# Operand addresses, GpSimd's share and the last norm columns of a hybrid decoder layer in float32

## Chip, cores and metric

The kernel runs on one core of a Trainium2 chip. The metric is device time in microseconds, from one execution to the next of the same program; less is better. A profiled execution has its own time, a little above those of the plain runs.

## What is computed

One decoder layer over 256 tokens of width 1,024, all in float32. Five branches read the same input x: block attention (a), a mixture of three dilated windows (b), forgetting attention (c), a gated delta rule (d) and cross-attention into 256 memory tokens (e). Each has six heads of 64 (e has four of 96).

```python
h = x @ w_in + b_in                       # q, k, v, gates z and merge logits of all branches
o = stack([o_a, o_b, o_c, o_d, o_e]) * silu(z)
y = einsum('bsnc,ncd->bsnd', o, w_branch)
y = sum(sigmoid(merge_logits) * y, axis=2) @ w_out
return layer_norm(DEEPNORM_ALPHA * x + y, ln_g, ln_b)
```

In branch b the three windows share one softmax: numerators and denominators of the three groups are added with a common maximum.

## The kernel before

**Split products.** A float32 operand is split into `hi` (rounded, by ScalarE) and `lo` (the rest, by VectorE; `split`, L122), and a product is three matmuls, hi by hi, hi by lo and lo by hi (`mm3`, L126). x is kept split for the whole kernel in `xhi` and `xlo`. Weights are streamed: a `Unit` (L163) loads up to 1,024 columns into a `raw` buffer on SP's queue, splits them into `hi` and `lo`, and its chunks issue the matmuls. A merge cycle has one unit of 24 products with x (256 wide, `mm<-xhi,hi`, `mm<-xhi,lo`, `mm<-xlo,hi`) and one of 9 products with a gated branch, whose operand lies in pool `f3` (`mm<-f,hi`, `mm<-f,lo`); there are five merges of eight cycles. The memory's keys (`mk`) are 72 products of the same width whose operand lies in `big` (`mm<-big,hi`, `mm<-big,lo`).

**Pools.** SBUF is given out in the order in which pools are opened (L79 to L83): `cpool` (constants, `xhi`, `xlo`, small tiles), `wpool` (`raw` x5, `hi` x4, `lo` x4, 4,096 bytes each), `f3` (16 tiles of 3,072 bytes), `big` (2 of 9,216), `sp`.

**Order.** The main loop (L1119) goes through the units. After each chunk `stepper` lets side streams (the attention branches, the delta rule, the memory norm) go on for a few steps. A planner then orders each engine's instructions by its own estimate of times; those passed to `keep` hold their order among themselves.

**The start.** The first four units are the weights of c's values (`wcs`, 402 columns); with each comes a quarter of x (`load_x`, `split_x`, L278 to L289), which takes a `raw` buffer for every two quarters. All loads are on SP's queue.

**Branch b** (`attend`, L724). For each of three head pairs and two heads the exponentials of three score groups are taken on ScalarE with the row sums as accumulators (L768), the three are added up on VectorE (L771), the row sums reduced and inverted (L775, L776), and the result is scaled (L781), transposed on TensorE (L787) and multiplied with v.

**The end.** `load_res` (L1077) loads the residual x and the norm's weights and scales the residual on ScalarE (L1086). The output product of 8 slices (k) is summed in PSUM: token tile 0 in two pieces of 512 columns, tile 1 in 512, 256 and 256 (`PC`, L1021). The pieces of a token tile lie in one two-bank tile (L1036); the last one has its own. `finish` (L1050) issues the last slices piece by piece, adds the residual (L1071), takes statistics (L1072), and `norm` applies the layer norm in two passes of VectorE over each half (L1062, L1063) and stores it.

Of the kernel before, what the change touches and what calls it, by code (L numbers as in the profile page):

```python
# [15 lines left out]
P = 128  # L16
S = 256
# [58 lines left out]
@with_exitstack  # L76
def kernel(ctx: ExitStack, tc: tile.TileContext, T: dict, out: bass.AP):
    nc = tc.nc
    cpool = ctx.enter_context(tc.tile_pool(name="cpool", bufs=1))  # L79
    wpool = ctx.enter_context(tc.tile_pool(name="wpool", bufs=3))  # L80
    f3 = ctx.enter_context(tc.tile_pool(name="f3", bufs=16))
    big = ctx.enter_context(tc.tile_pool(name="big", bufs=2))
    sp = ctx.enter_context(tc.tile_pool(name="sp", bufs=4))  # L83
    ps = ctx.enter_context(tc.tile_pool(name="ps", bufs=2, space=bass.MemoryType.PSUM))
    dr = ctx.enter_context(tc.tile_pool(name="dr", bufs=1, space=bass.MemoryType.DRAM))
# [33 lines left out]
        return pst("av", shape, 1)  # L119


    def split(hi, lo, src):  # L122
        A_.activation(hi, src, AF.Copy)  # L123
        V_.tensor_tensor(lo, src, hi.bitcast(F32), op=ALU.subtract)  # L124

    def mm3(pt, lh, ll, rh, rl, first, last, pin=False):  # L126
# [10 lines left out]
    HR = (slice(0, 64), slice(64, 128))  # L137


    xhi, xlo = ct("xhi", (P, KD, S), F32R), ct("xlo", (P, KD, S), F32R)  # L140
    cst = ct("cst", (P, C_N))
    vb, vcb = ct("vb", (P, 2, BW)), ct("vcb", (P, BW + 18))
    bcol = ct("bcol", (P, T["bcol"].shape[1]))
# [19 lines left out]
    class Unit:  # L163
# [7 lines left out]
        def load(self):  # L171
            self.r = wpool.tile([P, 1024], F32, tag="raw", name=nm("raw"), bufs=NRAW)
            for i, p in enumerate(self.parts):
                if self.before is not None:
                    self.before[0](i, len(self.parts))
                nc.sync.dma_start(self.r[:, p], self.src[:, p])

        def split(self):
            self.h = wpool.tile([P, 1024], F32R, tag="hi", name=nm("hi"), bufs=NHI)
            self.l = wpool.tile([P, 1024], F32R, tag="lo", name=nm("lo"), bufs=NHI)  # L180
            for i, p in enumerate(self.parts):
                if self.before is not None:
                    self.before[1](i, len(self.parts))
                split(self.h[:, p], self.l[:, p], self.r[:, p])

    def need(name):
        while name is not None and name not in done:
# [88 lines left out]
    xraw = {}  # L276

    def load_x(i, j, n):  # L278
        if i % 2 == 0 and j == 0:
            xraw["t"] = wpool.tile([P, 4, S], F32, tag="raw", name=nm("raw"), bufs=NRAW)  # L280
        w = 2 // n
        o = 2 * i + w * j
        xraw[i, j] = xraw["t"][:, o % 4:o % 4 + w]
        nc.sync.dma_start(xraw[i, j], T["xT"][:, o:o + w])

    def split_x(i, j, n):
        w = 2 // n
        o = 2 * i + w * j
        split(xhi[:, o:o + w], xlo[:, o:o + w], xraw[i, j])  # L289

    def evac_c(p, t):
        if t == 0:
# [10 lines left out]
    def consts():  # L303
        for _ in range(CW):
            yield 1
        nc.sync.dma_start(vcb, T["vcb"].to_broadcast([P, BW + 18]))
        nc.sync.dma_start(bcol, T["bcol"])
        nc.sync.dma_start(cw, T["convw"])
        nc.sync.dma_start(adt, T["adt"].to_broadcast([P, 12]))
        nc.sync.dma_start(cst[:, :C_MA], T["cst"][:, :C_MA])  # L310
        flag("consts")


# [6 lines left out]
    def scalars():  # L320

        yield from wait("sc")
        nc.sync.dma_start(cst[:, C_MA:], T["cst"][:, C_MA:])
        nc.sync.dma_start(gnw, T["gnw"])
        nc.sync.dma_start(mgb, T["mgb"])
        nc.sync.dma_start(vb, T["vb"].to_broadcast([P, 2, BW]))

        V_.tensor_scalar(cwh, cw, 0.5, None, op0=ALU.mult)
        hb = bcol[:, 3 * len(FM):]
        V_.tensor_scalar(hb, hb, 0.5, None, op0=ALU.mult)  # L330
        for n, f in [("z" + i, 0.5) for i in BR] + list(QSCALE.items()):
            i = FM.index(n) * 3
            V_.tensor_scalar(bcol[:, i:i + 3], bcol[:, i:i + 3], f, None, op0=ALU.mult)
        flag("bias")
        yield
        a, lp = ct("a", (P, 2, 12)), ct("lp", (P, 2, 12))
        e, s1, s2, ea = ct("e", (P, 24)), ct("s1", (P, 24)), ct("s2", (P, 24)), ct("ea", (P, 6))
        for t in range(2):
# [12 lines left out]
        V_.tensor_scalar(s1, e, 2.0, None, op0=ALU.add)  # L351
        V_.reciprocal(s1, s1)
        V_.tensor_tensor(s1, s1, e, op=ALU.mult)
        V_.tensor_tensor(s2, s1, s1, op=ALU.mult)
        V_.tensor_scalar(lpf, s2, 2.0 / 17, None, op0=ALU.mult)
        for n in (15, 13, 11, 9, 7, 5, 3):
            V_.scalar_tensor_tensor(lpf, lpf, 2.0 / n, s2, op0=ALU.add, op1=ALU.mult)
        V_.scalar_tensor_tensor(lpf, lpf, 2.0, s1, op0=ALU.add, op1=ALU.mult)
        V_.scalar_tensor_tensor(lpf, af, 0.0, lpf, op0=ALU.max, op1=ALU.add)
        yield  # L360

        for t in range(2):
# [361 lines left out]
    def attend(br, groups, vname, maskf, width):  # L724
# [5 lines left out]
        def pair(m):  # L730
# [33 lines left out]
            for g in range(ng):  # L764
                for x in range(2):
                    l = L[x][g]
                    for t, sl in SL:
                        A_.activation(l[:, sl], l[:, sl], AF.Exp, bias=mms[x][:, t:t + 1], scale=-1.0, accum_out=sm_[x][:, t, g:g + 1])  # L768
                    yield
                    if g:  # L770
                        V_.tensor_tensor(L[x][0], L[x][0], l, op=ALU.add)  # L771
            for x in range(2):
                rs = spt("rs", (P, 2), bufs=4)
                if ng > 1:
                    V_.tensor_reduce(rs, sm_[x], axis=AX.X, op=ALU.add)  # L775
                    V_.reciprocal(rs, rs)  # L776
                else:
                    V_.reciprocal(rs, sm_[x][:, :, 0])
                l = L[x][0]
                for t, sl in SL:  # L780
                    V_.tensor_scalar(l[:, sl], l[:, sl], rs[:, t:t + 1], None, op0=ALU.mult)  # L781
# [237 lines left out]
    def out_units():  # L1019
# [12 lines left out]

        def chunk(u, k, t):
            if k == 0 and t == 0:
                lgs = [lgps() for _ in range(2)]
                fin["p"] = [[lg[:, i] for i in range(2)] for lg in lgs]  # L1036
                fin["p"][1].append(mmps((P, 512)))
                warm = spt("warm", (P, 1), bufs=1)
                A_.activation(warm, yhl[2][0][:, 1, 0:1].bitcast(F32), AF.Sqrt, scale=0.0, bias=0.0)
# [10 lines left out]
        def finish():  # L1050
            xres, lngb = R["xres"], R["lngb"]
            st2 = [ct(f"st{t}", (P, len(PC[t]), 6)) for t in range(2)]

            def norm(t):
                V_.bn_aggr(mv[:, t], st2[t].rearrange("p c s -> p (c s)"))
                rs = rstd[:, t:t + 1]
                V_.tensor_scalar(rs, mv[:, t, 1:2], LN_EPS, None, op0=ALU.add)
                A_.activation(rs, rs, AF.Sqrt)
                V_.reciprocal(rs, rs)
                for c, cs in enumerate((slice(0, 512), slice(512, 1024))):  # L1060
                    o = xres[:, t, cs]
                    V_.scalar_tensor_tensor(o, o, mv[:, t, 0:1], lngb[:, 0, cs], op0=ALU.subtract, op1=ALU.mult)  # L1062
                    V_.scalar_tensor_tensor(o, o, rs, lngb[:, 1, cs], op0=ALU.mult, op1=ALU.add)  # L1063
                    (nc.sync, nc.scalar)[c].dma_start(out[t * P:(t + 1) * P, cs], o)
# [12 lines left out]
    def load_res():  # L1077
# [5 lines left out]
        for _ in range(8):  # L1083
            yield
        for t in range(2):
            A_.activation(xres[:, t], xres[:, t], AF.Copy, scale=ALPHA)  # L1086
            yield


    def block(n):  # L1090
# [122 lines left out]
```

## Time and profile before

| what | us |
|---|---|
| median of 3 runs | 467.25 (467.22 to 468.22) |
| the profiled execution | 469.32 |
| its span, first to last instruction | 467.2 |
| mean granted clock of TensorE | 0.994 |

In the views below, a row of busy times gives an engine, its busy time and its share of the span. In the timeline a row is a start, a duration, an engine, a line, an operation, output <- inputs with the matmul's rows*columns and output shape, and a count; "x2" merges two instructions in a row. `mm<-xhi,hi` is a matmul into PSUM tile `mm` from `xhi` and `hi`. Matmuls overlap, so their rate is read from starts, not from durations.

### The profile page before, as it was taken

To read this page: it belongs to the slowest core of one execution; us is meant where nothing else is said; L and a number is where in the kernel's file an instruction comes from. 1 tells how busy PE (TensorE), PEld (TensorE's weight loads), DVE (VectorE), ACT (ScalarE), POOL (GpSimd) and SP (SyncE) were. 2 spreads that over 40 slices of the span, in tenths; PEclk is the share of its full clock that TensorE was granted. 3 is DMA by queue.
4 is the path that set the end of the run, shared out by engine and by line. 5 is a ranking of instruction groups with operands and counts; after the bars stand their busy time and mean duration, and the time that the engine had idled before them with its cause. 6 is when DMAs were issued, how large, how long until landed. Compare 5 with 4: busy or idle time off the path is not lost. (4 is left out here: it accounts for less than half of the span.)

```text
span 467.2 us, 10262 instructions
## 1 busy us (share of the span) xinstructions
PE 449.9 (96%) x4039; PEld 425.0 (91%) x4039; DVE 328.1 (70%) x757; ACT 265.5 (57%) x520; POOL 30.6 (7%) x36
## 2 busy tenths in 40 slices
PE   6999999999999999999999989999989999999993
PEld 3999999999998999999999989988989999999963
DVE  4799998877797535564655689895676565587746
ACT  5466685765666644444434976694684654475600
POOL 0000020010000000000000112100022112200000
PEclk9899999999999999999999999999999999999999
DMA  7978577555445545566434165564765445678202
GB/s 253 380 246 255 164 225 252 159 178 173 125 130 160 152 125 172 176 202 183 125 109 126 60 176 182 173 193 152 250 201 184 145 150 148 190 234 278 91 0 90
DMA packets 35051, 81.38 MB, mean 174 GB/s; under 512 B 8970, under 2 KB 17468, under 8 KB 34876
## 3 DMA queue, kind: packets, MB, share of 16 engines
q1 hardware_dynamic: 34715, 80.22, 55.8%
q8 instruction: 31, 0.51, 0.4%
q10 hardware_dynamic: 288, 0.52, 0.3%
q14 instruction: 17, 0.13, 0.1%
HBM read 79.37 MB, written 1.36 MB: 173 GB/s over the span
## 5 line engine op out<-in xcount | busy, mean ns | idle before, releaser
L124 DVE TENSOR_TENSOR lo<-raw,hi 128x1024 fp32r<-128x1024 f32 (+4 forms) x163 | 169.3, 1040 | 83.4 <-ACT hi L123 80.8
L128 PE MATMUL mm<-xhi,hi 128*128 128x256 f32 x776 | 219.5, 283 | 1.2 <-DVE yt L993 1.2
L128 PE MATMUL mm<-xhi,lo 128*128 128x256 f32 x776 | 216.1, 279 | 1.3 <-DVE lo L124 1.3
L128 PE MATMUL mm<-xlo,hi 128*128 128x256 f32 x776 | 216.5, 279 | 0.0
L123 ACT ACTIVATE hi<-raw 128x1024 fp32r<-128x1024 f32 (+4 forms) x163 | 146.0, 899 | 111.9 <-PE mm L128 83.5
L128 PEld LDWEIGHTS mm<-xhi,hi 128*128 128x128 f32 x776 | 146.3, 189 | 5.8 <-issue 2.7
L128 PEld LDWEIGHTS mm<-xhi,lo 128*128 128x128 f32 x776 | 145.8, 188 | 1.8 <-DVE lo L124 1.7
L128 PEld LDWEIGHTS mm<-xlo,hi 128*128 128x128 f32 x776 | 146.0, 188 | 0.8 <-issue 0.8
L128 PE MATMUL mm<-f,hi 128*128 128x256 f32 x240 | 44.7, 282 | 0.7 <-ACT th L976 0.7
L994 POOL TENSOR_TENSOR yacc<-yacc,yt 128x256 f32<-128x256 f32 x24 | 24.4, 1018 | 280.0 <-DVE yt L993 275.2
L128 PEld LDWEIGHTS mm<-f,hi 128*128 128x128 f32 x240 | 36.6, 188 | 1.6 <-ACT th L976 1.3
L128 PE MATMUL mm<-f,lo 128*128 128x256 f32 x120 | 33.7, 281 | 0.0
L128 PEld LDWEIGHTS mm<-f,lo 128*128 128x128 f32 x120 | 22.6, 188 | 0.0
L128 PE MATMUL mm<-hi,xhi 128*128 128x384 f32 (+1 forms) x48 | 16.6, 363 | 2.1 <-ACT hi L123 2.1
L135 PE MATMUL lg<-f,f 64*128 64x256 f32 (+2 forms) x192 | 18.5, 354 | 0.0
L976 ACT ACTIVATE th<-mm,bcol 128x256 f32<-128x256 f32 x40 | 18.5, 462 | 0.0
L768 ACT ACTIVATE pr<-pr,mm 128x128 f32<-128x128 f32 (+1 forms) x36 | 15.9, 443 | 4.5 <-DVE mm L759 4.5
L128 PE MATMUL mm<-lo,xhi 128*128 128x384 f32 (+1 forms) x48 | 17.3, 360 | 0.4 <-DVE lo L124 0.4
L128 PE MATMUL mm<-hi,xlo 128*128 128x384 f32 (+1 forms) x48 | 17.0, 354 | 0.0
L123 ACT ACTIVATE f<-og 128x256 fp32r<-128x256 f32 x12 | 4.9, 416 | 19.3 <-DVE og L695 15.3
L705 ACT ACTIVATE f<-mm,bcol 128x256 f32<-128x256 f32 x33 | 15.1, 456 | 0.0
L135 PEld LDWEIGHTS lg<-f,f 64*128 64x128 f32 (+1 forms) x192 | 12.5, 186 | 2.6 <-issue 0.9
(221 smaller groups left out, 529.9 us busy)
## 6 DMA issues: line engine op xcount, KB each, us to landing
raw<-in_wf_dram SPq DMA_DIRECT2D x60, 512.0 KB, 4.3
raw<-in_wm_dram SPq DMA_DIRECT2D x40, 512.0 KB, 4.0
raw<-in_wb_dram SPq DMA_DIRECT2D x40, 192.0 KB, 2.5
raw<-in_wt_dram SPq DMA_DIRECT2D x12, 384.0 KB, 3.5
raw<-in_wo_dram SPq DMA_DIRECT2D x8, 512.0 KB, 4.1
gr<-gscr SPq DMA_DIRECT2D x12, 128.0 KB, 3.5
raw<-in_wcs_dram SPq DMA_DIRECT2D x3, 402.0 KB, 5.6
raw<-in_mem_dram SPq DMA_DIRECT2D x2, 512.0 KB, 4.8
```

Source lines behind the costliest of these rows:

```text
L123: A_.activation(hi, src, AF.Copy)
L124: V_.tensor_tensor(lo, src, hi.bitcast(F32), op=ALU.subtract)
L128: ins = PE.matmul(pt, l, r, start=start, stop=stop)
L135: keep(PE.matmul(pt, l, r, start=start, stop=stop))
L705: A_.activation(R[name][:, m], p, AF.Identity, bias=b, scale=1.0 if scale is None else scale)
L768: A_.activation(l[:, sl], l[:, sl], AF.Exp, bias=mms[x][:, t:t + 1], scale=-1.0, accum_out=sm_[x][:, t, g:g + 1])
L976: A_.activation(th, p, AF.Tanh, bias=bcol[:, i:i + 1], scale=0.5)
L994: (V_ if last else G_).tensor_tensor(yacc[:, d], yacc[:, d], yt, op=ALU.add)
```

## The change

Pools are opened in another order, with two pads, so that `wpool` and the tiles of `f3`, `big` and x get other addresses modulo 128. x is loaded into a tile of `big` and its first two pieces go to ScalarE's queue; these loads, the constants and the splits at the start are kept in order. In branch b row sums are taken by the fused last addition, the other addition goes to GpSimd. The residual is scaled by GpSimd in four pieces. The output pieces of a token tile lie in different PSUM tiles. In `norm` the last part (512 columns of token tile 0, 128 of tile 1) goes to ScalarE and GpSimd.

```diff
-    cpool = ctx.enter_context(tc.tile_pool(name="cpool", bufs=1))
+    xpool = ctx.enter_context(tc.tile_pool(name="xpool", bufs=1))
+    padw = ctx.enter_context(tc.tile_pool(name="padw", bufs=1))
     wpool = ctx.enter_context(tc.tile_pool(name="wpool", bufs=3))
+    padf = ctx.enter_context(tc.tile_pool(name="padf", bufs=1))
     f3 = ctx.enter_context(tc.tile_pool(name="f3", bufs=16))
     big = ctx.enter_context(tc.tile_pool(name="big", bufs=2))
+    cpool = ctx.enter_context(tc.tile_pool(name="cpool", bufs=1))
...
+    padw.tile([P, 16], F32, name="padw")
+    padf.tile([P, 112], F32, name="padf")
+    xhi, xlo = [xpool.tile([P, KD, S], F32R, name=n) for n in ("xhi", "xlo")]
...
     def load_x(i, j, n):
-        if i % 2 == 0 and j == 0:
-            xraw["t"] = wpool.tile([P, 4, S], F32, tag="raw", name=nm("raw"), bufs=NRAW)
+        if i == 0 and j == 0:
+            xraw["t"] = bigt([P, KD, S])
...
-        nc.sync.dma_start(xraw[i, j], T["xT"][:, o:o + w])
+        keep((nc.scalar if i == 0 else nc.sync).dma_start(xraw[i, j], T["xT"][:, o:o + w]))
...
-                        A_.activation(l[:, sl], l[:, sl], AF.Exp, bias=mms[x][:, t:t + 1], scale=-1.0, accum_out=sm_[x][:, t, g:g + 1])
+                        A_.activation(l[:, sl], l[:, sl], AF.Exp, bias=mms[x][:, t:t + 1], scale=-1.0,
+                                      accum_out=sm_[x][:, t, 0:1] if ng == 1 else None)
                     yield
-                    if g:
-                        V_.tensor_tensor(L[x][0], L[x][0], l, op=ALU.add)
+                    if 0 < g < ng - 1:
+                        G_.tensor_tensor(L[x][0], L[x][0], l, op=ALU.add)
+                    elif g:
+                        for t, sl in SL:
+                            V_.tensor_tensor_reduce(l[:, sl], L[x][0][:, sl], l[:, sl], 1.0, 0.0, ALU.add, ALU.add, sm_[x][:, t, 0:1])
+                        L[x][0] = l
...
-                fin["p"] = [[lg[:, i] for i in range(2)] for lg in lgs]
+                fin["p"] = [[lg[:, t_] for lg in lgs] for t_ in range(2)]
...
+                nb = nmr[:, t:t + 1]
+                V_.tensor_scalar(nb, rs, mv[:, t, 0:1], -1.0, op0=ALU.mult, op1=ALU.mult)
+                parts = ((0, 512), (512, 1024)) if t == 0 else ((0, 512), (512, 896), (896, 1024))
...
+                    if c == len(parts) - 1:
+                        A_.activation(o, o, AF.Identity, scale=rs, bias=nb)
+                        G_.tensor_tensor(o, o, lngb[:, 0, cs], op=ALU.mult)
+                        G_.tensor_tensor(o, o, lngb[:, 1, cs], op=ALU.add)
+                        (nc.scalar, nc.sync)[t].dma_start(out[t * P:(t + 1) * P, cs], o)
+                        continue
...
-            A_.activation(xres[:, t], xres[:, t], AF.Copy, scale=ALPHA)
-            yield
+            for c in range(2):
+                xr = xres[:, t, c * 512:(c + 1) * 512]
+                G_.tensor_scalar(xr, xr, ALPHA, None, op0=ALU.mult)
+                yield
```

## Rows read from the trace of the kernel before

**Rows 1.** Busy times of the page, TensorE first.

```profile
PE 449.9 (96%) x4039; PEld 425.0 (91%) x4039; DVE 328.1 (70%) x757; ACT 265.5 (57%) x520; POOL 30.6 (7%) x36
```

**Rows 2.** Waits of TensorE: total us, times, longest us.

```profile
PE lg L128 <- DVE big L1071: 1.6, 2, 0.8
```

**Rows 3.** Timeline of TensorE, one merge cycle and the start of the next.

```profile
393.63 0.29 PE L128 MATMUL mm<-xhi,hi 128*128 128x256 f32 x1
...
393.99 0.28 PE L128 MATMUL mm<-xhi,hi 128*128 128x256 f32 x1
...
396.37 0.39 PE L128 MATMUL mm<-f,hi 128*128 128x256 f32 x2
...
397.43 0.29 PE L128 MATMUL mm<-xhi,hi 128*128 128x256 f32 x1
```

**Rows 4.** Timeline of TensorE, the memory's keys.

```profile
312.06 0.52 PE L128 MATMUL mm<-big,hi 128*128 128x256 f32 x3
...
314.94 0.28 PE L128 MATMUL mm<-big,hi 128*128 128x256 f32 x1
```

**Rows 5.** Timeline of TensorE, products with x, then 512-wide output products.

```profile
62.49 0.28 PE L128 MATMUL mm<-xhi,hi 128*128 128x256 f32 x1
...
69.44 0.28 PE L128 MATMUL mm<-xhi,lo 128*128 128x256 f32 x1
...
450.58 0.39 PE L128 MATMUL lg<-lo,f 128*128 128x512 f32 x1
...
451.72 0.61 PE L128 MATMUL lg<-f,f 128*128 128x512 f32 x2
```

**Rows 6.** Chain that ended last: start us, us, what.

```profile
342.08 1.05 ACT big L1086
...
443.93 3.44 PE lg L128 x15
...
448.14 7.15 PE lg L128 x30
...
455.32 0.70 DVE big L1071
...
459.95 0.43 DVE big L1071
...
461.15 0.15 DVE rstd L1057
461.30 1.32 DVE big L1062 x2
```

**Rows 7.** Windows in branch b: length, busy time of each engine.

```profile
257.00:268.00 11.00, 10.42 (x91) 10.22 (x90) 7.36 (x20) 10.93 (x32) 1.80 (x2) 1.00 0.20 62
300.00:312.00 12.00, 11.27 (x95) 10.76 (x94) 10.42 (x27) 12.00 (x38) 0.00 (x0) 1.00 0.56 167
334.00:345.00 11.00, 9.57 (x81) 9.17 (x80) 6.75 (x20) 10.88 (x33) 0.75 (x1) 1.00 0.80 294
```

The columns of a window are PE, PEld, DVE, ACT and POOL busy, the granted clock, the DMA share and GB/s.

**Rows 8.** Groups by form: busy us, mean ns, idle before.

```profile
L771 DVE TENSOR_TENSOR pr<-pr,pr 128x384 f32<-128x384 f32 x12 | 6.6, 554 | 5.1 <-ACT pr L768 5.0
...
L768 ACT ACTIVATE pr<-pr,mm 128x128 f32<-128x128 f32 x18 | 7.0, 391 | 4.5 <-DVE mm L759 4.5
L768 ACT ACTIVATION_READ_ACCUMULATOR pr<-pr,mm 128x1 f32 x36 | 6.8, 188 | 0.0
```

**Rows 9.** Timeline of GpSimd: an addition alone, and one under VectorE.

```profile
266.00 0.75 POOL L994 TENSOR_TENSOR yacc<-yacc,yt 128x256 f32<-128x256 f32 x1 [6.89 <-DVE yt L993]
...
288.86 1.65 POOL L994 TENSOR_TENSOR yacc<-yacc,yt 128x256 f32<-128x256 f32 x1 [6.06 <-DVE yt L993]
```

**Rows 10.** Windows of the start.

```profile
7.00:9.70 2.70, 1.33 (x6) 0.69 (x5) 1.00 (x3) 1.55 (x3) 0.00 (x0) 1.00 1.01 379
9.70:11.00 1.30, 0.90 (x3) 0.57 (x4) 1.30 (x2) 0.92 (x2) 0.00 (x0) 1.00 1.05 402
11.00:14.00 3.00, 3.00 (x11) 2.97 (x10) 2.75 (x14) 1.90 (x3) 0.00 (x0) 0.51 1.08 323
```

More of the change, by code (lines that the diff above doesn't have):

```diff
@@ L119, in avps, with split @@
         return pst("av", shape, 1)
-    def split(hi, lo, src):
-        A_.activation(hi, src, AF.Copy)
+    def split(hi, lo, src, pin=False):
+        ins = A_.activation(hi, src, AF.Copy)
+        if pin:
+            keep(ins)
         V_.tensor_tensor(lo, src, hi.bitcast(F32), op=ALU.subtract)
@@ L137 @@
     HR = (slice(0, 64), slice(64, 128))
-    xhi, xlo = ct("xhi", (P, KD, S), F32R), ct("xlo", (P, KD, S), F32R)
+    padw.tile([P, 16], F32, name="padw")
+    padf.tile([P, 112], F32, name="padf")
+    xhi, xlo = [xpool.tile([P, KD, S], F32R, name=n) for n in ("xhi", "xlo")]
     cst = ct("cst", (P, C_N))
@@ L175, in load @@
                     self.before[0](i, len(self.parts))
-                nc.sync.dma_start(self.r[:, p], self.src[:, p])
+                ins = nc.sync.dma_start(self.r[:, p], self.src[:, p])
+                if self.before is not None:
+                    keep(ins)
         def split(self):
@@ L183, in split @@
                     self.before[1](i, len(self.parts))
-                split(self.h[:, p], self.l[:, p], self.r[:, p])
+                split(self.h[:, p], self.l[:, p], self.r[:, p], self.before is not None)
     def need(name):
@@ L278, in load_x @@
     def load_x(i, j, n):
-        if i % 2 == 0 and j == 0:
-            xraw["t"] = wpool.tile([P, 4, S], F32, tag="raw", name=nm("raw"), bufs=NRAW)
+        if i == 0 and j == 0:
+            xraw["t"] = bigt([P, KD, S])
         w = 2 // n
         o = 2 * i + w * j
-        xraw[i, j] = xraw["t"][:, o % 4:o % 4 + w]
-        nc.sync.dma_start(xraw[i, j], T["xT"][:, o:o + w])
+        xraw[i, j] = xraw["t"][:, o:o + w]
+        keep((nc.scalar if i == 0 else nc.sync).dma_start(xraw[i, j], T["xT"][:, o:o + w]))
     def split_x(i, j, n):
@@ L288, in split_x @@
         o = 2 * i + w * j
-        split(xhi[:, o:o + w], xlo[:, o:o + w], xraw[i, j])
+        split(xhi[:, o:o + w], xlo[:, o:o + w], xraw[i, j], True)
     def evac_c(p, t):
@@ L305, in consts @@
             yield 1
[L306 to L310, printed above, removed]
+        keep(nc.sync.dma_start(vcb, T["vcb"].to_broadcast([P, BW + 18])))
+        keep(nc.sync.dma_start(bcol, T["bcol"]))
+        keep(nc.sync.dma_start(cw, T["convw"]))
+        keep(nc.sync.dma_start(adt, T["adt"].to_broadcast([P, 12])))
+        keep(nc.sync.dma_start(cst[:, :C_MA], T["cst"][:, :C_MA]))
         flag("consts")
@@ L322, in scalars @@
         yield from wait("sc")
[L323 to L326, printed above, removed]
+        keep(nc.sync.dma_start(cst[:, C_MA:], T["cst"][:, C_MA:]))
+        keep(nc.sync.dma_start(gnw, T["gnw"]))
+        keep(nc.sync.dma_start(mgb, T["mgb"]))
+        keep(nc.sync.dma_start(vb, T["vb"].to_broadcast([P, 2, BW])))
         V_.tensor_scalar(cwh, cw, 0.5, None, op0=ALU.mult)
@@ L767, in pair @@
                     for t, sl in SL:
-                        A_.activation(l[:, sl], l[:, sl], AF.Exp, bias=mms[x][:, t:t + 1], scale=-1.0, accum_out=sm_[x][:, t, g:g + 1])
+                        A_.activation(l[:, sl], l[:, sl], AF.Exp, bias=mms[x][:, t:t + 1], scale=-1.0,
+                                      accum_out=sm_[x][:, t, 0:1] if ng == 1 else None)
                     yield
-                    if g:
-                        V_.tensor_tensor(L[x][0], L[x][0], l, op=ALU.add)
+                    if 0 < g < ng - 1:
[4 more added lines that the diff above has]
+                        L[x][0] = l
             for x in range(2):
                 rs = spt("rs", (P, 2), bufs=4)
[L774 to L778, printed above, removed]
+                V_.reciprocal(rs, sm_[x][:, :, 0])
                 l = L[x][0]
@@ L1052, in finish @@
             st2 = [ct(f"st{t}", (P, len(PC[t]), 6)) for t in range(2)]
+            nmr = ct("nmr", (P, 2))
             def norm(t):
@@ L1059, in norm @@
                 V_.reciprocal(rs, rs)
-                for c, cs in enumerate((slice(0, 512), slice(512, 1024))):
-                    o = xres[:, t, cs]
+                nb = nmr[:, t:t + 1]
+                V_.tensor_scalar(nb, rs, mv[:, t, 0:1], -1.0, op0=ALU.mult, op1=ALU.mult)
+                parts = ((0, 512), (512, 1024)) if t == 0 else ((0, 512), (512, 896), (896, 1024))
+                for c, (lo, hi) in enumerate(parts):
+                    cs = slice(lo, hi)
+                    o = xres[:, t, cs]
+                    if c == len(parts) - 1:
[4 more added lines that the diff above has]
+                        continue
                     V_.scalar_tensor_tensor(o, o, mv[:, t, 0:1], lngb[:, 0, cs], op0=ALU.subtract, op1=ALU.mult)
```

## Prediction

> **What bounds the kernel now.** Read the page's busy times first: TensorE 96% against 70% for VectorE and 57% for ScalarE [rows 1]. So the span is the sum of the matmuls' start-to-start times plus the places where TensorE stands still, and only what changes one of the two counts. Five places are to be read.
>
> 1. The merge stage, 40 cycles of 24 products with x (`mm<-xhi,hi` and its two companions) and 9 with a gated branch (`mm<-f,hi`), in TensorE's timeline [rows 3]. A cycle lasts 397.43 - 393.63 = 3.80 us. From 393.99 on, products with x start every (396.37 - 393.99) / 21 = 0.1133 us; the 9 with the branch take (397.43 - 396.37) / 9 = 0.1178; and the first three with x after them take 0.36 together, again 0.12 each.
> 2. The memory keys, the same 256-wide shape with the operand in `big`: 25 starts between 312.06 and 314.94, 24 steps of 0.1200 us [rows 4].
> 3. Why the two rates? In the program before, the allocator puts `xhi`, `xlo` at byte 16,512 (0 modulo 128) and all of `wpool` from 62,144 on (64 modulo 128); `f3` and `big` follow it in whole multiples of 128 and are at 64 too. So weights and x are already 64 bytes apart; weights against branch, memory or the merged y are 0 apart. The fast rate goes with 64, the slow one with 0. But the trace also has long stretches of x products at 64 apart that run slow: 59 steps from 62.49 to 69.44, 0.1178 us each [rows 5]. 512-wide products at 0 apart start every 1.14 / 5 = 0.228 us [rows 5], which is two fast 256-wide steps.
> 4. The chain of waits at the end [rows 6]: TensorE stops at 447.37, VectorE reads one half of a PSUM tile for 0.70 us, and only then TensorE goes on at 448.14 with the other half of the same tile. At 455.3 it happens again; the waits of TensorE put it at 1.6 us in two [rows 2].
> 5. Three stretches where TensorE idles in mid-kernel [rows 7]: 0.58, 0.73 and 1.43 us, just where ScalarE is busy 10.93 of 11.00, 12.00 of 12.00 and 10.88 of 11.00 us. They are the three head pairs of branch b.
>
> [...]
>
> **The change, part by part.**
>
> *Addresses.* `xpool` first (16,384 bytes), a pad of 64, `wpool` in multiples of 4,096, a pad of 448: x stays at 0, weights at 64, but `f3` and `big` move to 0. Products with x keep their distance. Those that gain it: 360 merge products, 72 of the memory keys, 36 256-wide of the output. The late output units (k = 6, 7) have both operands in `f3` and stay 0 apart. If all run at the fast rate, a merge cycle of 33 takes 33 x 0.1133 = 3.74 instead of 3.80: 0.06 x 40 = 2.4 us; the keys 72 x 0.0067 = 0.5; the output products 36 x 0.0067 = 0.2. The 512-wide ones are already at two fast steps: 0. Together 3.1. The other end: they fall into the slow mode that the x products show at 64 apart, 0.1178, and gain only 72 + 36 times 0.0022 = 0.2. I take 2.9, because in the merge stage itself the x products always come back to the fast rate.
>
> [...]
>
> *PSUM tiles of the output* (`fin["p"]`). The two halves of one token tile now lie in two tiles, so the second half no longer waits for the read of the first. Each stop is 448.14 - 447.37 = 0.77 plus the overlap lost at a restart, 0.39 - 0.23 = 0.16 [rows 5, 6]: 0.93, twice, 1.9 us. What is late next there is nothing: each half has 15 products, 3.4 us, against 0.70 of reading and as much for statistics. The other end is 1.6, the idle alone.
>
> *Branch b's softmax and the residual.* ScalarE loses 36 accumulator reads of 188 ns, 12 or 2.26 us in each pair [rows 8], and the two residual scalings of 1.05 us, which stand in the chain at 341 to 343, in the third stretch [rows 6]. VectorE loses six of twelve additions (554 ns, [rows 8]) and turns the others into two fused instructions each. GpSimd gets six additions of 384 columns and four scalings. Relief of 2.26 us, or 4.3 in the third pair, is more than each idle time (0.58, 0.73, 1.43), so all 2.74 could go; at the other end ScalarE's order stays and 0 goes. I take 2.6. A GpSimd addition of 256 columns lasts 0.75 us alone and 1.65 behind a VectorE instruction with two SBUF inputs [rows 9]; for 384 columns that is at most 2.5, and it lies beside the exponentials of the next score group (for two heads 4 x 0.4 us), so I cost it at nothing; without that cover it is the rival below. The residual is read only from 447 on.
>
> *Start.* The first two pieces of x go to ScalarE's queue, so SP issues each later transfer two slots earlier, and x no longer takes two of the five `raw` buffers. But the bytes ahead of the second weight unit are the same and the transfers are near their limit (DMA share 1.01, 379 GB/s, [rows 10]). Bounds: 0 and 3.3 (1.77 of idle plus half of 3 us at the low clock). I take 0.6. The `keep` on DMAs and splits adds no instruction and is costed at nothing: what it can hold up stands in the start, within those bounds.
>
> *Tail.* For the last token tile VectorE's two passes cover 896 columns, not 1,024: two instructions of 384 columns (0.55) in place of 512 (0.70) save 0.30, and the new product for the bias costs 0.15 [rows 6, 8]. The other 128 columns go through ScalarE (0.39) and two GpSimd operations between half of 0.75 and 1.65 us each. They end between 0.15 earlier and 1.3 later than VectorE does now. I take 0.2 later.
>
> Sum: -2.9 - 1.9 - 2.6 - 0.6 + 0.2 = -7.8. The profiled execution took 469.32 (span 467.2 and 2.1 around it), so 461.5 there; the median of the runs, 467.25, is 2.07 below it: **459.4 us**.
>
> **Rivals.**
>
> - *Distance does nothing*: both rates are modes that a run falls into by what went before. For it: the slow stretch at 64 apart [rows 5]; against: the steady 0.1200 of the keys over a long run [rows 4]. 459.4 + 2.9 = 462.3. [...]
> - *GpSimd and VectorE shut each other out in the tail.* The GpSimd addition of 0.75 took 1.65 when it began under a VectorE instruction [rows 9], and the last passes of VectorE also read two SBUF operands. Then both tail operations wait: 1.3 instead of 0.2, 460.5. [...]
> - *The start clears.* No idle, no stretch at the low clock: 3.3 instead of 0.6, 456.7. Against it is the DMA share.
> - *Slower: GpSimd's additions hold up the transposes of branch b.* These are pinned in TensorE's order, so whatever is late there stops it. Place: three pairs; price: up to two additions of 1.65 per pair, 9.9 us, and the 2.6 of relief not had: 459.4 + 12.5 = 471.9. It decides from a stop of 1.7 us per pair on (7.8 - 2.6 = 5.2 over three). Against: the longest wait of TensorE for another engine's result at the end is 0.8 us [rows 2], and where b's pairs run the idle sums to 2.74 in all [rows 7].
>
> **How the numbers follow.** Forecast 0.60 (456.5 to 461.5), distance nothing 0.20 (to 463.8), tail lock 0.07, start clears 0.07 (from 455.5), additions in the way 0.06, of which a third ends level. The time is that of the forecast; 456.0 to 463.8 leaves out the last case and part of the fourth. About 0.2% is what these runs can tell from no change. Faster 0.94, same 0.02, slower 0.04.
>
> **What would show it.** Right: `mm<-f,hi` at 0.113 and merge cycles of 3.74; keys at 0.113; no wait of TensorE for the read of `lg` at L1071's successor; TensorE idle under 0.2 in each of the three stretches; the wait for GpSimd absent from TensorE's list. Wrong: merge cycles still of 3.80; transposes of branch b waiting; a GpSimd operation in the chain that ends last, more than 1 us after VectorE's last pass; a longer low-clock stretch at the start.

## The result and the profile after

The changed kernel takes 461.96 us (median of 4 runs, 460.41 to 462.43); the kernel before took 467.74 on the same chip. The ratio is 0.9842, 95% interval 0.9816 to 0.9869: 1.6% faster. The prediction was 459.4, so 2.6 us of the 7.8 did not come: the time lies inside the stated range (456.0 to 463.8), but above the forecast's own band (456.5 to 461.5), where the prediction had put its rival "distance does nothing". The profiled execution took 462.43, its span 460.6 against 467.2.

Marks in TensorE's timeline (all in us from the span's start) say where the 6.6 us lie. The 360 products with a gated branch count the five merges, 72 each; "f 72" is the first of the second merge. The end of the last product is put 0.12 after its start.

| stretch | before | after | difference |
|---|---|---|---|
| start, to the first product of 256 columns with x | 18.60 | 16.09 | -2.51 |
| to f 0 | 152.27 | 153.49 | +1.22 |
| f 0 to f 72 | 78.46 | 77.97 | -0.49 |
| f 72 to f 144 (b's first two pairs, memory) | 85.66 | 81.38 | -4.28 |
| f 144 to f 216 (b's third pair) | 36.69 | 38.49 | +1.80 |
| f 216 to the output | 63.74 | 63.29 | -0.45 |
| output products | 24.33 | 22.13 | -2.20 |
| from there to the end | 7.44 | 7.77 | +0.33 |

Each column is one execution. In the seven traces that keep the change's start and addresses the stretch to f 0 takes 152.7 to 153.8, so a difference of half a microsecond in one row says little.

Two rows stand out: one in which time was given back (+1.80) and one that should have gained and lost (+1.22).

Busy times of the page, and the waits of TensorE, which answer to [rows 1, 2]:

```profile
PE 447.2 (97%) x4039; PEld 424.5 (92%) x4039; DVE 325.7 (71%) x763; ACT 262.1 (57%) x484; POOL 51.5 (11%) x50
```

```profile
PE lg L800 <- DVE pr L794: 1.6, 1, 1.6
PE mm L135 <- ACT hi L128: 1.2, 1, 1.2
...
PE mm L135 <- ACT th L989: 0.8, 1, 0.8
PE mm L135 <- DVE yt L1006: 0.5, 1, 0.5
```

The wait for the read of an output tile, 1.6 us in two before, is gone. A new one heads the list: transposes of branch b (L800) wait 1.6 us for VectorE's scaling of the softmax (L794).

**The merge cycle** of [rows 3], in TensorE's timeline:

```profile
393.31 0.28 PE L135 MATMUL mm<-xhi,hi 128*128 128x256 f32 x1
...
396.04 0.39 PE L135 MATMUL mm<-f,hi 128*128 128x256 f32 x2
...
397.06 0.28 PE L135 MATMUL mm<-xhi,hi 128*128 128x256 f32 x1
```

It lasts 3.75 instead of 3.80, and the 9 products with the branch take 1.02 / 9 = 0.1133: the predicted picture. **The memory's keys** [rows 4] show another:

```profile
305.24 0.40 PE L135 MATMUL mm<-big,hi 128*128 128x256 f32 x2
...
310.90 0.28 PE L135 MATMUL mm<-big,lo 128*128 128x256 f32 x1
311.11 0.65 PE L142 MATMUL av<-pT,f 128*64 128x256 f32 x4
...
312.72 0.28 PE L135 MATMUL mm<-big,lo 128*128 128x256 f32 x1
...
313.86 0.28 PE L135 MATMUL mm<-big,lo 128*128 128x256 f32 x1
```

Up to 310.90 there are 48 steps of 0.1179; then attention's products (`av`) cut in; after them 10 steps of 0.114. The same operands at the same addresses run here at either rate, 0.1179 ahead of the interruption and 0.114 behind it.

**Branch b's windows** [rows 7]:

```profile
257.00:268.00 11.00, 11.00 (x98) 10.89 (x97) 8.72 (x25) 9.64 (x19) 3.47 (x5) 1.00 0.37 112
300.00:312.00 12.00, 12.00 (x102) 11.36 (x101) 11.40 (x25) 7.87 (x16) 0.00 (x0) 1.00 0.58 184
...
334.00:345.00 11.00, 9.27 (x78) 8.76 (x76) 7.99 (x19) 5.07 (x10) 8.90 (x7) 1.00 0.46 152
```

In the first two TensorE no longer idles (from 96 to 314 us it has no stop of 0.1 us or more). In the third it idles 1.73, though ScalarE is busy only 5.07: GpSimd is busy 8.90 of 11. The timeline there, all engines:

```profile
335.84 3.50 POOL L1116 TENSOR_SCALAR big<-big 128x512 f32<-128x512 f32 x2
...
339.32 1.99 POOL L784 TENSOR_TENSOR pr<-pr,pr 128x384 f32<-128x384 f32 x2
340.37 1.09 DVE L787 CUSTOM_DVE_ANT_0 pr<-pr,pr 128x128 f32<-128x128 f32 x1 [2.94 <-POOL pr L784]
...
342.56 0.42 DVE L794 TENSOR_SCALAR pr<-pr,rs 128x128 f32<-128x128 f32 x1
342.90 0.28 DVE L787 CUSTOM_DVE_ANT_0 pr<-pr,pr 128x128 f32<-128x128 f32 x1
...
343.04 0.33 PE L800 MATMUL lg<-cst,pr 128*128 128x128 f32 x1 [1.60 <-DVE pr L794]
```

Read it from the bottom. The transpose waits for the scaled softmax; that for the fused addition; that, 2.94 us, for GpSimd's addition (L784); and GpSimd begins it at the moment when the last scaling of the residual (L1116) is done. The planner put all four scalings ahead of it in GpSimd's queue. A smaller part is the fused addition itself: begun while GpSimd works on its second addition it takes 1.09 us, and its twin of the same size at 342.90, with GpSimd idle, 0.28.

**The start** [rows 10]:

```profile
4.80:9.00 4.20, 3.44 (x10) 3.30 (x11) 2.92 (x6) 3.09 (x7) 0.00 (x0) 1.00 1.04 354
9.00:11.40 2.40, 2.40 (x14) 2.28 (x14) 1.83 (x3) 2.00 (x3) 0.00 (x0) 1.00 1.04 416
11.40:14.00 2.60, 2.60 (x16) 2.57 (x15) 2.10 (x3) 1.77 (x2) 0.00 (x0) 1.00 1.04 406
```

The first weight product comes 0.76 later (5.57 against 4.81), but from 9.00 on TensorE has no idle time and, at a granted clock of 1.00, no low stretch as in [rows 10] (0.51 for 3.00 us).

### The profile page after: what moved, and what is told of

Its sections match the earlier page's. It is cut to its first block, busy times and chain, and to the rows that moved or that the text cites. A ratio compares the mean times of both kernels' runs of the same rounds, so it can differ in the third digit from the quotient of the medians.

```text
span 460.6 us, 10256 instructions
## 1 busy us (share of the span) xinstructions
PE 447.2 (97%) x4039; PEld 424.5 (92%) x4039; DVE 325.7 (71%) x763; ACT 262.1 (57%) x484; POOL 51.5 (11%) x50
## 4 chain that ended last, share of the span: by engine, by line
PE 91%; DVE 3%; POOL 2%; DMA 2%; ACT 1%; issue 0%; POOLq 0%; DVEq 0%; ACTq 0%
PE mm L135 75%; PE lg L135 4%; PE lg L142 4%; PE av L142 2%; POOL big L1116 1%; PE lg L800 1%; DMA mf<-gscr 1%; DMA big<-in_xT_dram 1%; PE lg L653 1%; DVE lo L131 1%; DVE pr L794 0%; POOL pr L784 0%; PE lg L875 0%; ACT pr L779 0%; PE lg L943 0%
## 5 line engine op out<-in xcount | busy, mean ns | idle before, releaser
L131 DVE TENSOR_TENSOR lo<-raw,hi 128x1024 fp32r<-128x1024 f32 (+4 forms) x163 | 167.1, 1026 | 84.6 <-ACT hi L128 81.4
L128 ACT ACTIVATE hi<-raw 128x1024 fp32r<-128x1024 f32 (+4 forms) x163 | 146.3, 899 | 115.0 <-PE mm L135 85.8
L1007 POOL TENSOR_TENSOR yacc<-yacc,yt 128x256 f32<-128x256 f32 x24 | 26.6, 1109 | 220.6 <-DVE yt L1006 208.6
L135 PE MATMUL mm<-hi,xhi 128*128 128x384 f32 (+1 forms) x48 | 16.5, 363 | 1.2 <-ACT hi L128 1.2
L499 POOL TENSOR_SCALAR_AFFINE_SELECT pr<-pr 128x256 f32<-128x256 f32 x6 | 6.4, 1066 | 94.3 <-DVE pr L498 76.3
L763 DVE CUSTOM_DVE_ANT_0 pr<-lg,cst 128x128 f32<-128x128 f32 (+1 forms) x48 | 14.1, 352 | 1.0 <-PE lg L142 1.0
```

Source lines behind the costliest of these rows:

```text
L128: ins = A_.activation(hi, src, AF.Copy)
L135: ins = PE.matmul(pt, l, r, start=start, stop=stop)
L499: G_.affine_select(E[:, 0::2], E[:, 0::2], pattern=[[0, 2], [1, P]], compare_op=ALU.is_ge, fill=-BIG, base=0, channel_multiplier=-1)
L763: V_.tensor_tensor_reduce(l[:, sl], pts[x][:, sl], mk[x][:, sl], 1.0, 3.0e38, ALU.add, ALU.min, mx[x][:, t, g:g + 1])
L1007: (V_ if last else G_).tensor_tensor(yacc[:, d], yacc[:, d], yt, op=ALU.add)
```

## Experiments

All are compared with the kernel before on the same chip, and stage by stage in the trace. Rates come from counting: a start-to-start step of 100 to 130 ns between two 256-wide products counts, some 2,620 in each execution. A step belongs to the operand of the product that begins it. A return from the branch's products to products with x counts as fast if the median of the fourth to eighth step behind it is under 115.5 ns (the first three take 0.12 each in [rows 3]).

| kernel | x, f3 and big from the weights, bytes | mean step with x / branch / memory, ns | steps with x under 116 ns |
|---|---|---|---|
| before | 64; 0 | 114.8 / 118.0 / 119.7 | 1,542 of 2,209 |
| after | 64; 64 | 115.3 / 114.6 / 116.9 | 1,265 of 2,205 |
| e_addr_only | 64; 64 | 115.6 / 115.8 / 116.7 | 1,099 of 2,209 |
| e_f3_same | 64; 0 | 115.2 / 118.2 / 119.8 | 1,322 of 2,206 |
| e_all_same | 0; 0 | 118.7 / 119.0 / 119.8 | 398 of 2,208 |
| e_d32 | 32; 32 | 118.3 / 118.3 / 118.2 | 106 of 2,208 |
| e_d192 | 192; 192 (modulo 256) | 117.6 / 117.5 / 117.8 | 83 of 2,206 |

**Addresses alone** (e_addr_only): the kernel before with the pools and pads of the change, the rest as before.

```diff
-    cpool = ctx.enter_context(tc.tile_pool(name="cpool", bufs=1))
+    xpool = ctx.enter_context(tc.tile_pool(name="xpool", bufs=1))
+    padw = ctx.enter_context(tc.tile_pool(name="padw", bufs=1))
...
+    padw.tile([P, 16], F32, name="padw")
+    padf.tile([P, 112], F32, name="padf")
```

> The kernel before with the pools and pads of the change and nothing else, so every engine's instructions are those of before. If distance modulo 128 counts: merge cycles of 3.74 instead of 3.80 us, branch products at 0.113 us; 40 cycles by 0.06 and a little in the output, so 2.4 to 2.8 us less than before (span about 464.6), stops of TensorE as before. If distance does nothing (both rates are modes that a run falls into): 467.2 as before, cycles of 3.80.

Measured: 469.27, ratio 1.0009 (0.9984 to 1.0033), span 468.7. Alone, this part gains nothing. TensorE's timeline shows a cycle falling from one rate to the other:

```profile
388.48 0.28 PE L131 MATMUL mm<-f,lo 128*128 128x256 f32 x1
388.68 1.52 PE L138 MATMUL av<-pT,f 128*32 128x128 f32 x48
390.13 0.38 PE L131 MATMUL mm<-xhi,hi 128*128 128x256 f32 x1
390.35 0.28 PE L131 MATMUL mm<-xlo,hi 128*128 128x256 f32 x1
...
393.06 0.40 PE L131 MATMUL mm<-f,hi 128*128 128x256 f32 x2
...
394.12 0.28 PE L131 MATMUL mm<-xhi,hi 128*128 128x256 f32 x1
```

After the `av` products 23 steps take (393.06 - 390.35) / 23 = 0.1178, the 9 with the branch 0.1178 too, and so it stays in the eleven cycles that follow. In the kernel before, of 32 returns from products with the branch to products with x, 30 ran fast; here 14 of 32.

**Branch and memory at distance 0 again** (e_f3_same): after, with `padf.tile([P, 128]` in place of 112.

> The changed kernel with a second pad of 512 instead of 448 bytes: f3 and big lie at 64 modulo 128, 0 apart from the weights, as before the change. Distance: merge cycles back to 3.80 us, keys at 0.120, 2.4 to 2.8 us more than the changed kernel (span about 463.2). Modes: no difference.

Measured: 463.69, ratio 0.9890 (0.9862 to 0.9919), span 462.8. The branch's products are back at 118.2 and the keys at 119.8; all 33 returns to x are fast. By the steps it loses 302.8 - 301.3 = 1.5 us (2,616 and 2,615 steps, so 1.4 for the same number), by the span 2.2. The wider pad also moves `cpool` and `sp`, which lie behind it, by 64 bytes; what that does is not separated.

**Everything at distance 0** (e_all_same): `padw` of 32 and `padf` of 128 floats.

> The changed kernel with pads of 128 and 512 bytes: x, weights, f3 and big all at 0 modulo 128. The suspected cost is laid on all 2,328 products with x too. Distance: all of them at 0.120 us, some 1,550 that ran at 0.1133 and 590 that ran at 0.118: 1,550 x 0.0067 + 590 x 0.002 = 11.5 us more, and the branch products' 2.6: about 14 us above the changed kernel (span 474 to 475). Modes: no difference from the changed kernel.

Measured: 469.35, ratio 1.0013 (0.9992 to 1.0033), span 467.8, 7.2 more than after. A merge cycle there:

```profile
406.43 0.28 PE L135 MATMUL mm<-xhi,hi 128*128 128x256 f32 x1
...
409.28 0.40 PE L135 MATMUL mm<-f,hi 128*128 128x256 f32 x2
```

24 steps in 2.85: 0.119. The whole gain of the change is undone by this alone, so distance counts; but the span grows by half of the 14 us expected. By the mean step it is (118.8 - 115.2) ns x 2,620 = 9.4 us; 2.5 us of idle time go in return, most of it the stop of 1.60 before branch b's transposes, which TensorE, later there, does not meet.

**Distance 32** (e_d32): pads of 8 and 120 floats; every engine's order is that of after.

> The kernel after with pads of 32 and 480 bytes: x, f3 and big stay at 0 modulo 128, the weights go to 32, so that all operands of the products are 32 bytes apart instead of 64; every engine's order is the same as in after. Theory (the 256-wide rate hangs on the distance: 0.120 at 0 apart, 0.1133 or 0.1178 at 64): at 32 it lies between, some 0.117 to 0.120, at most 1 in 5 of the starts under 0.116, span 460.6 + 3 to 8. Rival (any distance other than 0 does the same): as after, more than half of the starts under 0.116, span 460.6 give or take 1. Second rival (distance has no part in it, the rates are modes): also as after, but then the variant with everything 0 apart, which measured 972 of 2,237 starts at 0.120, stays unexplained.

Measured: 468.68, ratio 0.9991 (0.9973 to 1.0010), span 466.0. As expected from distance, 118.2 to 118.3 ns in all three families, against 114.6 to 116.9 in after. So 32 bytes, a distance other than 0, were not enough.

**Distance 192** (e_d192): pads of 48 and 80 floats.

> The kernel after with pads of 192 and 320 bytes: weights at 192 bytes, x, f3 and big at 0 modulo 256, so 64 apart modulo 128 as in after, but 64 on the other side modulo 256; every engine's order is that of after. Theory (the distance counts modulo 128): as after, 1,100 to 1,400 of the 2,230 starts of products with x under 0.116, span 460.6 give or take 1. Rival (the distance counts modulo 256 or more, so that 192 is another case than 64): a mix unlike that of after, fewer than 800 or more than 1,700 of the starts under 0.116, and 2 us or more of difference.

Measured: 466.83, ratio 0.9978 (0.9959 to 0.9997), span 465.2. The rival holds: 192 is not 64, though both are 64 modulo 128. Nor is it the weights' own place that counts: they are at 192 modulo 256 here and in the kernel before (62,144), where 1,542 of 2,209 steps with x are fast. Yet the fast rate exists at 192 too, in TensorE's timeline 1.4 us after a wait of 0.61:

```profile
338.69 0.38 PE L135 MATMUL mm<-xhi,hi 128*128 128x256 f32 x1
338.91 0.28 PE L135 MATMUL mm<-xlo,hi 128*128 128x256 f32 x1
...
341.51 0.39 PE L135 MATMUL mm<-f,hi 128*128 128x256 f32 x2
```

23 steps in 2.60: 0.113, kept through the branch's products up to the next interruption at 345.4. So at 192 both rates occurred and the fast one seldom (83 of 2,206 steps); at 64 half of the steps (e_addr_only) to 70% (before) had it.

**Scalings later** (e_res_late): the loop of scalings placed behind `yield from wait("ogb")`, that is, after branch b in program order.

> The changed kernel, but the residual's four scalings on GpSimd wait until branch b is done. If the stop of 1.6 us before the transposes of b's third pair comes from GpSimd's queue (four scalings of 1.9 us ahead of two additions): it goes, with the 0.45 us behind it, about 2.2 us less than the changed kernel (span about 458.4). If the additions on GpSimd are too slow by themselves: the stop stays over 1 us and the time is within 0.5 of the changed kernel.

Measured: 461.19, ratio 0.9838 (0.9807 to 0.9868), span 461.2. GpSimd's timeline shows that nothing was tested: the planner moved the scalings forward again.

```profile
332.65 7.11 POOL L1115 TENSOR_SCALAR big<-big 128x512 f32<-128x512 f32 x4 [33.74 <-issue]
339.73 1.98 POOL L784 TENSOR_TENSOR pr<-pr,pr 128x384 f32<-128x384 f32 x2
```

**No scaling at all** (e_res_fold): the layer norm does not change when its input is divided by ALPHA and its epsilon by ALPHA squared.

```diff
-                G_.tensor_scalar(xr, xr, ALPHA, None, op0=ALU.mult)
...
-    V_.scalar_tensor_tensor(o, fin["p"][t][i][:, :hi - lo], 0.5, o, ...)
+    V_.scalar_tensor_tensor(o, fin["p"][t][i][:, :hi - lo], 0.5 / ALPHA, o, ...)
-                V_.tensor_scalar(rs, mv[:, t, 1:2], LN_EPS, None, op0=ALU.add)
+                V_.tensor_scalar(rs, mv[:, t, 1:2], LN_EPS / ALPHA ** 2, None, op0=ALU.add)
```

> The kernel after without any residual scaling: the norm's inputs are divided by ALPHA throughout (the products are read with 0.5 / ALPHA, the epsilon is divided by ALPHA squared), so that GpSimd has only branch b's additions and the four scalings of 1.9 us are gone. Theory (the scalings queue ahead of the third pair's additions on GpSimd, and b's pinned transposes wait for them): the stop of 1.6 us before the transposes and the one of 0.45 behind it go; from f-product 144 to 216 the time falls from 38.49 by about 1.8 to 36.7, span 460.6 - 1.8 = 458.8. Rival (the additions themselves, 1.0 us each on GpSimd and blocked fused ones on VectorE, are late whatever is queued ahead): a stop of 1 us or more stays at the same transposes, span 460.6.

Measured: 459.66, ratio 0.9812 (0.9786 to 0.9839), span 457.8. f 144 to f 216 takes 36.62, 1.87 less than after. GpSimd's timeline, then the waits of TensorE:

```profile
329.41 1.99 POOL L784 TENSOR_TENSOR pr<-pr,pr 128x384 f32<-128x384 f32 x2 [31.95 <-ACT pr L779]
```

```profile
PE mm L135 <- ACT th L989: 1.3, 2, 0.8
```

The addition starts as soon as ScalarE has delivered, the wait of L800 is gone, and what is left is a wait for ScalarE's tanh. Only the removed scalings and the planner's new order behind them differ, and in the kernel after the addition begins as the last scaling ends, so the queue is shown as the cause. This version has the shortest span; its interval overlaps that of after.

**Scaling on ScalarE** (e_res_act): the two `A_.activation(xres[:, t], xres[:, t], AF.Copy, scale=ALPHA)` of before in place of GpSimd's four.

> The kernel after with the residual scaled by ScalarE in two instructions, as before. Theory (GpSimd's queue): the stop of 1.6 us before the third pair's transposes goes, because the additions no longer stand behind scalings, and ScalarE's two instructions of 1.05 us bring back at most the 0.7 of idle that the kernel before had there: 0.9 to 1.8 less than after, span 458.8 to 459.7. Rival (ScalarE was what held up the third pair before, and the scalings there cost as much as they do on GpSimd): no gain, 460.6 or more, with the stop now behind an exponential.

Measured: 461.81, ratio 0.9855 (0.9829 to 0.9881), span 460.3. The third pair's wait at L800 is gone, but another grows. Timelines of ScalarE and TensorE, then two windows:

```profile
332.59 1.04 ACT L1114 ACTIVATE big<-big 128x1024 f32<-128x1024 f32 x1
333.54 0.45 ACT L989 ACTIVATE th<-mm,bcol 128x256 f32<-128x256 f32 x1
```

```profile
334.04 0.50 PE L135 MATMUL mm<-f,hi 128*128 128x256 f32 x2 [1.79 <-ACT th L989]
```

```profile
334.00:335.10 1.10, 1.06 (x9) 1.06 (x9) 1.10 (x4) 1.10 (x2) 0.00 (x0) 1.00 0.16 66
335.10:338.50 3.40, 3.33 (x17) 3.04 (x16) 2.93 (x6) 1.97 (x4) 1.45 (x2) 0.50 0.64 183
```

A scaling stands ahead of the tanh that TensorE waits for: 1.79 against 0.84. Behind that stop 3.4 us run at a granted clock of 0.50, with products 0.214 apart. The rival was right on the total, by a mechanism that it did not have in full.

**The start as before** (e_start_undone): x in the `raw` buffers, all on SP's queue, no `keep`.

```diff
-            xraw["t"] = bigt([P, KD, S])
+            xraw["t"] = wpool.tile([P, 4, S], F32, tag="raw", name=nm("raw"), bufs=NRAW)
...
-        keep((nc.scalar if i == 0 else nc.sync).dma_start(xraw[i, j], T["xT"][:, o:o + w]))
+        nc.sync.dma_start(xraw[i, j], T["xT"][:, o:o + w])
```

> The kernel after with the start as before: pieces of x in the raw buffers and all on SP's queue, nothing pinned. Theory (the queues and buffers of the start are worth the 2.5 us by which the first product of the stage behind the start came earlier, 18.60 to 16.09): that product is back at 18.3 to 18.9, idle of 1.4 and 0.4 us and about 3 us at the low clock are back, span 460.6 + 2.5 = 463.1. Rival (the low clock in the start falls by chance, whatever the queues): the idle of 1.8 us comes back but the low stretch need not; the product at 16.5 to 17.5, span 461 to 462.

Measured: 463.13, ratio 0.9875 (0.9844 to 0.9907), span 461.7. The first product of the next stage is at 18.59, where it was before. Waits and a window of the start:

```profile
PE mm L135 <- ACT hi L128: 2.2, 3, 1.5
```

```profile
11.40:14.80 3.40, 3.40 (x12) 3.36 (x12) 3.37 (x16) 1.95 (x3) 0.00 (x0) 0.50 1.03 301
```

The idle time and the low clock come back together: the 2.5 us are the start's. Queue, buffers and kept order are taken back together, so which of them does it is open. The span grew by only 1.1 because TensorE, now 2.5 later, comes to branch b's third pair when the additions behind the scalings are done: the transposes start at 343.95 against 343.04, without a wait, and f 144 to f 216 takes 37.25.

**One PSUM tile for a token tile** (e_psum_undone): `fin["p"]` as before.

> The kernel after with the two halves of one token tile of the output in one PSUM tile, as before. Theory (the second half waits until VectorE has read the first): two stops of about 0.8 us and 0.16 of restart each come back, from the first output product to TensorE's end 22.13 + 1.9 = 24.0, span 462.5. Rival (the stops of before were caused by what VectorE still had to do there, not by the tile): one stop or none, 22.1 to 23.1, span 460.6 to 461.6.

Measured: 463.91, ratio 0.9899 (0.9869 to 0.9930), span 462.3. Output products take 24.24, 2.1 more, and the wait is back:

```profile
PE lg L135 <- DVE big L1099: 1.6, 2, 0.8
```

**Softmax of branch b as before**, without scaling (e_b_old): accumulators on ScalarE, twelve additions on VectorE.

```diff
-                    if 0 < g < ng - 1:
-                        G_.tensor_tensor(L[x][0], L[x][0], l, op=ALU.add)
-                    elif g:
...
+                    if g:
+                        V_.tensor_tensor(L[x][0], L[x][0], l, op=ALU.add)
```

> The kernel without residual scaling, with branch b's softmax as before: 36 accumulator reads on ScalarE, twelve whole additions on VectorE, none on GpSimd. Theory (ScalarE held up b's three pairs, and relief of 2.26 us a pair removes the stops): the stops of 0.58, 1.2 and 0.58 us in the first two pairs are back, the third has less than before because the scalings are gone too; from f-product 72 to 216 (117.8 us in the kernel without scaling) 2 to 4 us more, span 460 to 462. Rival (the stops went because the planner put b's pairs elsewhere, not because ScalarE has less to do): under 1 us more, span 458 to 459.

Measured: 464.70, ratio 0.9925 (0.9899 to 0.9950), span 463.5, 5.7 more than without scaling: f 72 to f 144 takes 87.13 against 81.22, f 144 to f 216 35.88 against 36.62. More than expected, and mostly not for the reason given. Of b's own stops the first pair's is back with 0.69, the second pair has none, and the third has 0.80 where the kernel without scaling has 0.84 and 0.42. The largest is this, in the timeline of all engines:

```profile
275.21 1.29 DVE L855 BATCH_NORM_STATS2 st<-raw 128x6 f32<-128x512 f32 x2 [3.18 <-DMA raw<-in_mem_dram]
...
276.42 0.40 DVE L1004 SCALAR_TENSOR_TENSOR yt<-th,mm 128x256 f32<-128x256 f32 x1
...
276.87 0.39 PE L135 MATMUL mm<-xhi,hi 128*128 128x256 f32 x1 [2.42 <-DVE yt L1004]
```

VectorE stands 3.18 us before the memory's statistics, whose data has not come, with the reading of a product tile queued behind; then 3.4 us at the low clock follow (277.36 to 280.78; 0.57 is the mean of 277 to 281), with products 0.21 apart, which costs half of that. The kernel before has the same stop, 1.20 us at 277.50. So the difference is 0.85 from the first pair (with 0.16 for the restart), 2.6 from the memory's stop, 1.7 from the clock and 0.5 before the memory's values (0.67 against 0.19), and 0.74 back in the third pair; some 0.5 lies ahead of f 72, where the softmax has no part. That is nearer to the rival: what b's softmax itself holds up is small, and what the planner then puts elsewhere is large.

**Norm as before**, without scaling (e_best): two passes of 512 on VectorE for each token tile.

> The kernel without residual scaling (products read with 0.5 / ALPHA) and with the norm's passes as before: two of 512 columns on VectorE for each token tile, nothing of it on ScalarE or GpSimd. Theory (the change's tail costs 0.33 us: 7.44 before, 7.77 after, because the second GpSimd operation ends later than VectorE's passes): from TensorE's end to the end of the span 7.4, span 457.8 - 0.35 = 457.5, ratio about 0.0008 below that of the kernel without scaling, which is less than the interval. Rival (VectorE's two longer passes cost what GpSimd's end saves, and the 0.33 came from the transfers): 7.8 as in after.

Measured: 460.83, ratio 0.9841 (0.9810 to 0.9871), span 459.4; from the last product to the end 7.81, not 7.4 (7.76 in the kernel without scaling). The theory falls: the 0.33 us of the tail are not the norm's columns. The span is 1.6 us above that kernel's, all of it ahead of the output products, which the norm does not touch: so much two kernels can differ for other reasons in one execution each.

## Why the prediction came out as it did

**Addresses: forecast -2.9, measured -0.4.** All counted steps have a mean of 302.4 / 2,621 = 0.1154 us before and 301.3 / 2,615 = 0.1152 after, times 2,620. Two steps failed. The first is "because in the merge stage itself the x products always come back to the fast rate". They did so behind products at distance 0: 30 of 32 and 33 of 33 returns were fast there (before, e_f3_same), but 14 of 32 and 26 of 33 behind products at 64 (e_addr_only, after). So branch and keys gained (118.0 to 114.6, 119.7 to 116.9 ns), and x from f 0 on did not (114.7 and 114.6). The second is "Products with x keep their distance", by which x outside the merges was put at nothing. Ahead of f 0, where no branch product stands, x went from 115.0 to 116.1 ns over 965 steps, about 1.0 of the +1.22. Most of that is one run, in TensorE's timeline, before and then after:

```profile
25.05 0.28 PE L128 MATMUL mm<-xhi,hi 128*128 128x256 f32 x1
...
48.98 0.28 PE L128 MATMUL mm<-xhi,hi 128*128 128x256 f32 x1
```

```profile
19.14 0.28 PE L135 MATMUL mm<-xlo,hi 128*128 128x256 f32 x1
...
50.59 0.28 PE L135 MATMUL mm<-xlo,hi 128*128 128x256 f32 x1
```

These are 211 steps of 0.1134 and 267 of 0.1178. Where all operands are 64 apart, none of the runs of 15 or more counted steps changes its rate on the way (48 runs in after, 51 in e_addr_only; in the kernel before, with the branch at 0, 18 of 51 do). So the rate that a long run takes at its start decides: the last 394 steps of the merges go at 113.4 ns in after and at 117.8 in e_addr_only. Against the 115.1 of the kernel before that is 0.7 us gained, which is the forecast's 0.06 for each of these twelve cycles, or 1.0 lost. It is not chance from one execution to the next: in all eight traces of the changed kernel and its variants with these addresses the first long run is slow and the last one fast.

Within the changed order the part is worth 1.4 us by the steps and 2.2 by the span (e_f3_same). The rival "distance does nothing" is refuted by e_all_same, 7.2 us, though its time, 462.3, came nearest; its reason, that a run falls into a rate by what went before, is right within one distance. What in an interruption picks the rate stays open.

**PSUM tiles: forecast -1.9, measured -2.2** by the output stage, 2.1 by the run that undoes it. Right.

**Softmax and residual: forecast -2.6, measured -4.28 + 1.80 = -2.5.** Some 0.5 of it are the rates'. The sum is near, its parts are not. In the first two pairs the idle 0.58 and 0.73 went, as forecast; but e_b_old, with the old softmax, has only the first of them, so that the new softmax is shown as the cause for one, and the planner's order is as likely for the other. Not foreseen: the stop of 1.20 behind the memory's statistics, and some 0.5 before the memory's values, went too. Not foreseen either: the third pair did not give 1.43 but has stops of 0.84, 1.60 and 0.45. The step that failed is "The residual is read only from 447 on", as the cover of the scalings: it asked who waits for their result and not what is queued behind them. They take 1.9 us each in the mean, 1.49 where no VectorE instruction overlaps and 2.05 and 2.56 where they begin under VectorE's subtraction with two SBUF inputs (L131), and the two additions of the third pair stood behind 7.5 us of them.

```profile
L1116 POOL TENSOR_SCALAR big<-big 128x512 f32<-128x512 f32 x4 | 7.5, 1897 | 33.3 <-issue 33.3
```

e_res_fold settles it. The rival "GpSimd's additions hold up the transposes" had place and sign, in one pair of three; but an addition takes 1.0 us, and what was late was mainly its start; the two fused additions beside GpSimd's work took 1.09 and 0.93 for 0.28 and 0.41, 1.3 us of the delay. In e_res_fold the first of them takes 1.09 too, but 8 us ahead of the transposes, and costs nothing.

**Start: forecast -0.6, measured -2.5.** The rival "the start clears" (3.3, which is 1.37 + 0.40 us of idle and half of 3.00 us at a granted clock of 0.51, [rows 10]) came closer. The failed step is that a DMA share above 1 leaves nothing to win: it was 1.01 to 1.08 [rows 10] and is still 1.04, but with the new queues, buffers and order TensorE starts 0.76 later and doesn't stop. In six of the other ten traces with the new start it does stop, 0.3 to 1.3 us in all between 8 and 13 us, but none of them has the low clock, and the first product with x comes at 15.9 to 16.5 in all eleven; in the three with the old start it comes at 18.6 to 18.7, behind 3.4 us at the low clock each time. So the low clock, 3.4 us at 0.50 and thus by estimate some 1.7, is the larger and the steady part of the gain.

**Tail: forecast +0.2, measured +0.33,** for another reason than given. Before, VectorE ended 4.39 after the last product and the end came 3.05 later; after, GpSimd ended 5.08 after it and the end came 2.69 later. With the norm undone it is 4.40 and 3.41. What takes 0.36 more than before behind the same last store is open, in one execution each.

```profile
455.82 1.27 DVE L1091 SCALAR_TENSOR_TENSOR big<-big,rstd,big 128x512 f32<-128x512 f32 x2
...
456.51 0.89 POOL L1086 TENSOR_TENSOR big<-big,big 128x128 f32<-128x128 f32 x1 [4.02 <-ACT big L1085]
...
457.48 0.45 POOL L1087 TENSOR_TENSOR big<-big,big 128x128 f32<-128x128 f32 x1
```

The rival in the tail is seen in kind: the first GpSimd operation, begun under VectorE's pass, takes 0.89, the second of the same size, with VectorE idle, 0.45; in token tile 0, at 512 columns each, the two took 1.30 and 1.29. It costs 0.44, not 1.1. The 0.75 of [rows 9] was begun with VectorE idle, which set in 0.39 later.

That the addresses' miss and the start's gain nearly cancel is luck. The 2.6 us that are missing: 1.2 in the spans (6.6 against 7.8), where the addresses gave 2.5 less and the start 1.9 more than forecast; the rest lies between the profiled executions, which differ by 6.9, and the medians, which differ by 5.8 in the one comparison and 5.3 against the 467.25 from which the forecast was reckoned.

## What to carry to other kernels

Work that nobody waits for still stands in a queue: before moving it to an idle engine, look at what the planner will put behind it, and ask first whether it can be folded away. Where one shape shows two rates, find out from the trace whether the rate belongs to the operands or to the run of instructions before selling a gain per instruction; here it was both. Undo each part alone in the changed program too: the start's 2.5 us became 1.1 there, since a later TensorE hid another stop.

## What the runs showed of the hardware

- 256-wide float32 products started every 0.113, 0.118 or 0.120 us. With weights 64 bytes behind the other operand (modulo 256) the first two occurred (1,265 of 2,205 steps with x under 116 ns in after, 1,099 of 2,209 in e_addr_only), with 32 hardly the first (106 of 2,208), with 192 the same (83 of 2,206); with 0 the mean was 118.7 ns (e_all_same). Where all operands were 64 apart (after, e_addr_only), a rate once taken stayed to the end of the run, up to 394 products, across a change of operand.
- GpSimd's scaling of 128x512 with one input took 1.49 us with VectorE idle, longer than its multiplication and its addition of the same size with two inputs, 1.30 and 1.29 (L1086 and L1087 in the output stage); begun under a VectorE subtraction with two SBUF inputs it took 2.05 and 2.56.
- VectorE's fused addition of 128x128 took 1.09 us begun under GpSimd's addition (L784), and 0.28 with GpSimd idle (340.37 and 342.90 in after).
- Stops of 1.79 and 2.42 us in mid-kernel (e_res_act, e_b_old) were followed by 3.4 us at a granted clock of 0.50; one of 1.60 (after) was not.
